# A decoder block's layer norm by running sums: statistics gathered per convolution group instead of after the convolution

## The chip, the cores and the metric

The kernel runs on one core of one Trainium2 chip. The metric is the device time of one execution in microseconds, lower is better. Five engines take part: TensorE (PE; its weight loads are PEld) multiplies matrices, VectorE (DVE) and ScalarE (ACT) work on elements, GpSimd (POOL) sets constants, and SyncE (SP) issues most of the loads. Every engine works through its own list of instructions in order and waits on semaphores for the others.

## What is computed

One hybrid decoder block over 256 tokens of 2048 channels. A combined projection feeds sparse attention and a causal convolution branch; both are gated, merged, projected by w_out and added to x through an adaLN gate g1; a gated MLP with a short convolution follows. The convolution branch is what the change touches:

```python
def conformer_conv(glu_in, w_dw, b_dw, ln_g, ln_b, w_pw, b_pw):
    a, g = jnp.split(glu_in, 2, axis=-1)
    u = a * jax.nn.sigmoid(g)
    u = causal_dwconv(u, w_dw, b_dw)                 # width 31, per channel
    u = jax.nn.silu(layernorm(u, ln_g, ln_b))        # over the 2048 channels of each token
    return u @ w_pw + b_pw

def layernorm(x, g, b):
    mu = jnp.mean(xf, axis=-1, keepdims=True)
    var = jnp.mean(jnp.square(xf - mu), axis=-1, keepdims=True)
    return (xf - mu) * lax.rsqrt(var + EPS) * g + b
```

## The kernel before

**Weight stream.** All large products run on weights streamed from memory in tiles of 128x1024 (512 KB). `wtile` (line 213) loads one into `raw` from SP's queue, ScalarE rounds it to `hi` (line 221), VectorE subtracts to get `lo` (line 222), and TensorE multiplies hi and lo parts with an activation that is split the same way (`split`, lines 344 and 345): 24 matmuls of 256 columns a tile in `sum_w` (lines 255 to 258), or as many of 512 columns for two tiles' worth of rows in `prod_x` (lines 243 to 245). There are four raw buffers and three each of hi and lo.

**Side work and its account.** Attention heads (`heads_q`), the convolution with its layer norm (`conv_q`) and the adaLN projections (`ada_q`) are queues of small steps. After each weight tile `tick` (line 122) adds to an account of each engine's time and gives out steps while no engine that the step costs is ahead of TensorE's account. A weight tile counts 2816 ns for TensorE (line 233) and 1217 for VectorE (line 223). `give` lets the step's instructions follow the `lo` of the tile before on VectorE (`issue_after`). `drain` gives all that is left. While `norm_only` is set and conv_q has steps, ada_q gets none.

**The convolution.** Channels lie in 16 blocks of 128 partitions; `u` holds all of them as [128, 16, 256]. Blocks are convolved in groups of three, the last one alone (`conv_blocks`, line 527): some taps are one VectorE instruction per block (line 543), the others a product on ScalarE per block (line 553) and one wide addition on VectorE for the group (line 562). The last addition writes the group back into u (line 560). The accumulator `cacc` has two buffers.

**The layer norm** comes after the last group, all through conv_q: `ln_mean1` to `ln_mean4` add the blocks up and a matmul with a matrix of ones sums over partitions; four `ln_centre` subtract the mean, square on ScalarE and fold (`half_sum`, lines 869 and 870); `ln_var` gets the reciprocal root; four `ln_scale` (line 917), eight `ln_silu` (line 923) and four `ln_split` end in uT, the activation of the next product, conv_pw_w (from line 961). Temporaries come from four buffers with the tag t4, also used by attention, by the products of the convolution and by the adaLN sums.

**What stands around it.** While the layer norm runs, TensorE does the products of the merge gates (line 952, four of eight tiles each). Then `drain(conv_q)`, the four products on conv_pw_w, and w_out in five chunks (line 1000) with `residual` behind each, which multiplies by g1b (line 990). g1b is the adaLN gate: 32 steps of ada_q, each a 512 KB piece of w_ada loaded into one of two `araw` buffers and a multiply-add on VectorE (lines 292 and 295), then products with ones and line 321. `conv_done` puts these 32 at the head of ada_q, since their result lies where the convolution's buffers were. What of them is left after the products on conv_pw_w is forced out by lines 972 and 973. Accumulators of w_out have two buffers, so the third chunk needs residual 0 done.

Of the kernel before, what the change touches and what calls it, by code (L numbers as in the profile page):

```python
# [9 lines left out]
F32 = mybir.dt.float32  # L10
F32R = mybir.dt.float32r
AF = mybir.ActivationFunctionType
ALU = mybir.AluOpType
# [3 lines left out]
P = 128  # L17
D = 2048
T = 256
# [12 lines left out]
EPS = 1e-6  # L32
# [15 lines left out]
LN_SILU = 1500  # L48
# [11 lines left out]
def block_kernel(ctx, tc, x, c, w_ada, b_ada, norm1_g, w_in, cmp_pe, w_kc1, w_kc2, w_vc1, w_vc2,  # L60
# [19 lines left out]
    def nm(s):  # L80
        n_[0] += 1
        return f"{s}_{n_[0]}"

    def t4(shape, dt=F32):
        return tmp.tile(shape, dt, tag="t4", name=nm("t4"))

    def pt(shape):
        return ps_t.tile(shape, F32, tag="pt", name=nm("pt"))
# [48 lines left out]
    def give(q):  # L137
        cost, f = q.popleft()
        use(**cost)
        with ExitStack() as es:  # L140
            es.enter_context(tc.issue_after(los[0]))
            if q is heads_q:
                es.enter_context(tc.high_priority(HP))
            f()

# [378 lines left out]

    MANY, FEW = tuple(s for s in range(2, CW) if s % 6) + (1,), tuple(range(6, CW, 4)) + (1,)

    def conv_blocks(b0, n, WIDE):

        box = {}
        blk = range(b0, b0 + n)  # L530

        def first(b):
            def f():
                if b == b0:
                    box["a"] = cvp.tile([P, n, T], F32, tag="cacc", name=nm("cacc"), bufs=2)
                nc.scalar.activation(box["a"][:, b - b0, :], u[:, b, :], AF.Identity, bias=cvb[:, b:b + 1],
                                     scale=cw[:, CW - 1, b:b + 1])
            return f

        def tap(b, s):  # L540
            def f():
                acc = box["a"][:, b - b0, s:]
                nc.vector.scalar_tensor_tensor(acc, u[:, b, :T - s], cw[:, CW - 1 - s, b:b + 1], acc,  # L543
                                               op0=ALU.mult, op1=ALU.add)
            return f

        def product(b, s):
            def f():
                if b == b0:
                    box["p"] = tmp.tile([P, n, T], F32, tag="t4", name=nm("cprod"))  # L550
                    if s == 1:
                        nc.gpsimd.memset(box["p"][:, :, 0:1], 0.0)
                nc.scalar.mul(box["p"][:, b - b0, s:], u[:, b, :T - s], cw[:, CW - 1 - s, b:b + 1])  # L553
            return f

        def wide(s):
            def f():
                acc, prod = box["a"], box["p"]
                if s == 1:
                    nc.vector.tensor_add(u[:, b0:b0 + n, :], acc, prod)  # L560
                else:
                    nc.vector.tensor_add(acc[:, :, s:], acc[:, :, s:], prod[:, :, s:])  # L562
            return f

        conv_q.extend(({"act": 600}, first(b)) for b in blk)
        narrow = deque(({"dve": 470}, tap(b, s)) for s in range(2, CW) if s not in WIDE for b in blk)
        each = -(-len(narrow) // len(WIDE))
        for s in WIDE:
            conv_q.extend(narrow.popleft() for _ in range(min(each, len(narrow))))
            conv_q.extend(({"act": 500}, product(b, s)) for b in blk)  # L570
            conv_q.append(({"dve": 170 + n * 265}, wide(s)))


    load.update(pe=0.0, dve=0.0, act=0.0, dma=0.0)
# [277 lines left out]
    def conv_done():  # L852

        cv.__exit__(None, None, None)
        norm_only[0] = True
        late = ctx.enter_context(tc.tile_pool(name="late", bufs=1))
        gate1["b"] = late.tile([P, D], F32, name="gb", tag="gb")
        gate1["rest"] = len(ada_q)
        for i in range(2):
            ada_q.extendleft(reversed(ada_steps(2 * D + i * WT, to_bcast(gate1["b"], 2 * D, i), 1500)))  # L860

    conv_q.append(({}, conv_done))


    lb = {}

    def half_sum(dst, a):

        nc.vector.tensor_add(a[:, 0:2, :], a[:, 0:2, :], a[:, 2:4, :])
        nc.vector.tensor_add(dst, a[:, 0, :], a[:, 1, :])  # L870

    def ln_mean1():
        lb["a"] = t4([P, 4, T])
        nc.vector.tensor_add(lb["a"], u[:, 0:4, :], u[:, 4:8, :])

    def ln_mean2():
        nc.vector.tensor_add(lb["a"], lb["a"], u[:, 8:12, :])

    def ln_mean3():
        nc.vector.tensor_add(lb["a"], lb["a"], u[:, 12:16, :])  # L880

    def ln_mean4():
        half_sum(lb["a"][:, 0, :], lb["a"])
        mp = pt([P, T])
        nc.tensor.matmul(mp, ones, lb["a"][:, 0, :], start=True, stop=True)
        lb["m"] = mp
        lb["q"] = t4([P, 4, T])

    def ln_centre(j):
        def f():  # L890
            v = u[:, 4 * j:4 * j + 4, :]
            nc.vector.scalar_tensor_tensor(v, lb["m"][:, None, :].to_broadcast([P, 4, T]), -1.0 / D, v,
                                           op0=ALU.mult, op1=ALU.add)
            s4 = t4([P, 4, T])
            nc.scalar.activation(s4, v, AF.Square)
            half_sum(lb["q"][:, j, :], s4)
        return f

    def ln_var():
        q = lb["q"]  # L900
        half_sum(q[:, 0, :], q)
        vp = pt([P, T])
        nc.tensor.matmul(vp, ones, q[:, 0, :], start=True, stop=True)
        ve = t4([P, 4, T])
        nc.vector.tensor_scalar(ve[:, 0, :], vp, 1.0 / D, EPS, op0=ALU.mult, op1=ALU.add)
        nc.scalar.activation(ve[:, 1, :], ve[:, 0, :], AF.Sqrt)
        nc.vector.reciprocal(ve[:, 2, :], ve[:, 1, :])
        nc.vector.tensor_mul(ve[:, 3, :], ve[:, 2, :], ve[:, 2, :])
        nc.vector.tensor_mul(ve[:, 3, :], ve[:, 3, :], ve[:, 0, :])
        nc.vector.tensor_scalar(ve[:, 3, :], ve[:, 3, :], -0.5, 1.5, op0=ALU.mult, op1=ALU.add)  # L910
        nc.vector.tensor_mul(ve[:, 3, :], ve[:, 3, :], ve[:, 2, :])
        lb["r"] = ve[:, 3, :]

    def ln_scale(j):
        def f():
            v = u[:, 4 * j:4 * j + 4, :]
            nc.vector.tensor_tensor(v, v, lb["r"][:, None, :].to_broadcast([P, 4, T]), op=ALU.mult)
        return f

# [6 lines left out]
    def ln_split(j):  # L926
        def f():
            if j == 0:
# [2 lines left out]
            split(lb["uT"][:, s], u[:, s, :])  # L931
        return f

    conv_q.extend(({"dve": d, "act": a}, f) for d, a, f in
                  [(1130, 0, ln_mean1), (1130, 0, ln_mean2), (1130, 0, ln_mean3), (900, 0, ln_mean4)]
                  + [(2000, 1050, ln_centre(j)) for j in range(4)] + [(3000, 1700, ln_var)]
                  + [(1130, 0, ln_scale(0))]
                  + [i for j in range(4) for i in [(1130, 0, ln_scale(j + 1))] * (j < 3)
                     + [(0, LN_SILU, ln_silu(4 * j)), (0, LN_SILU, ln_silu(4 * j + 2))]])


    merged = bigt([P, KB, T])
# [178 lines left out]
```

## Time and profile before

| | |
|---|---|
| runs | 1758.6, 1765.0, 1765.9 us (median 1765.0) |
| the profiled execution | 1765.5 us, span 1763.7 us |
| busy share of the span | PE 97%, PEld 88%, DVE 74%, ACT 56%, POOL 0% |
| mean granted TensorE clock | 0.98 |
| loads | 403 MB, 230 GB/s over the span |

The share of an engine is an average over the whole span; what matters for a change is the stretch where it acts. Here that is 227 us (the convolution starts) to 1000 us (w_out ends). The profile's page gives the shares, its lists name the waits, the windows give busy time and clock for a stretch, and the timelines show single instructions.

### The profile page before, as it was taken

The numbers are of one execution on the slowest core, as the hardware profiler recorded it, in microseconds if no ns is written. First come the engines' busy times: TensorE is split into PE (matmuls) and PEld (weight loads), VectorE is DVE, ScalarE is ACT, GpSimd is POOL, SyncE is SP. The second block draws the span as 40 slices with busy tenths as digits, with TensorE's granted clock in tenths as the row PEclk, the third lists the DMA queues.
The fourth block names the chain that finished last, engine by engine and source line by source line (L and its number), as shares of the span: only waits on it lengthen the run. The fifth ranks groups of instructions, "written<-read, shape, count | busy, mean of one in ns | idle before, by whom it ended". The sixth has DMA issues, their size and how long they took to land.

```text
span 1763.7 us, 29535 instructions
## 1 busy us (share of the span) xinstructions
PE 1703.1 (97%) x11652; PEld 1548.2 (88%) x11652; DVE 1313.1 (74%) x1722; ACT 991.5 (56%) x1506; POOL 6.2 (0%) x28
## 2 busy tenths in 40 slices
PE   6999999999999999996999899999999999999997
PEld 4899999999999999996987888888988888898886
DVE  2677798898887799887897677776577776576665
ACT  4443576885768767754434465554455554345553
POOL 0000000000000000000000000000000000000000
PEclk8999999999999999997999999999999999999998
DMA  9999788876556466767888667776777765666663
GB/s 343 328 350 318 240 272 273 268 247 217 157 174 185 143 212 202 221 217 274 305 296 308 199 216 226 226 225 221 224 225 220 223 211 183 191 191 188 188 193 124
DMA packets 263798, 406.82 MB, mean 231 GB/s; under 512 B 12620, under 2 KB 156780, under 8 KB 263020
## 3 DMA queue, kind: packets, MB, share of 16 engines
q1 hardware_dynamic: 261676, 399.44, 70.8%
q10 hardware_dynamic: 1984, 5.51, 0.9%
q8 instruction: 91, 1.49, 0.4%
q14 instruction: 47, 0.39, 0.1%
HBM read 402.80 MB, written 2.10 MB: 230 GB/s over the span
## 4 chain that ended last, share of the span: by engine, by line
PE 90%; DMA 5%; DVE 3%; issue 1%; ACT 1%; SPq 0%; DVEq 0%; ACTq 0%
PE accp L276 19%; PE accw L255 12%; PE accw L258 12%; PE accw L257 12%; PE accp L277 9%; PE accx L244 6%; PE accx L243 6%; PE accx L245 6%; DMA araw<-in_w_ada_dram 4%; PE pt L782 1%; DVE t L295 1%; PE pt L415 1%; PE pt L821 1%; DVE lo L222 1%; DMA araw<-in_w_kc_dram 1%
## 5 line engine op out<-in xcount | busy, mean ns | idle before, releaser
L221 ACT CAST hi<-raw 128x1024 fp32r<-128x1024 f32 x546 | 571.8, 1048 | 636.8 <-PE accw L257 196.9
L222 DVE TENSOR_TENSOR lo<-raw,hi 128x1024 fp32r<-128x1024 f32 x546 | 665.5, 1221 | 319.0 <-ACT hi L221 317.5
L255 PE MATMUL accw<-act,hi 128*128 128x256 f32 x1920 | 554.1, 289 | 21.7 <-ACT act L344 19.5
L257 PE MATMUL accw<-act,hi 128*128 128x256 f32 x1920 | 556.4, 290 | 1.5 <-DVE act L345 1.5
L258 PE MATMUL accw<-act,lo 128*128 128x256 f32 x1920 | 552.2, 288 | 0.7 <-DVE lo L222 0.7
L276 PE MATMUL accp<-act,hi 128*128 128x512 f32 x1408 | 492.3, 395 | 0.0
L255 PEld LDWEIGHTS accw<-act,hi 128*128 128x128 f32 x1920 | 374.0, 195 | 29.6 <-ACT act L344 21.0
L277 PE MATMUL accp<-act,lo 128*128 128x256 f32 x1408 | 393.3, 279 | 0.0
L257 PEld LDWEIGHTS accw<-act,hi 128*128 128x128 f32 x1920 | 373.8, 195 | 7.5 <-issue 4.9
L258 PEld LDWEIGHTS accw<-act,lo 128*128 128x128 f32 x1920 | 373.5, 195 | 6.8 <-issue 4.8
L276 PEld LDWEIGHTS accp<-act,hi 128*128 128x128 f32 x1408 | 264.0, 188 | 62.1 <-DVE act L345 0.3
L277 PEld LDWEIGHTS accp<-act,lo 128*128 128x128 f32 x1408 | 265.5, 189 | 0.2
L244 PE MATMUL accx<-lo,act 128*128 128x512 f32 (+2 forms) x664 | 228.9, 345 | 1.8 <-DVE lo L222 1.8
L243 PE MATMUL accx<-hi,act 128*128 128x512 f32 (+2 forms) x664 | 227.0, 342 | 0.0
L245 PE MATMUL accx<-hi,act 128*128 128x512 f32 (+2 forms) x664 | 226.8, 342 | 0.0
L295 DVE SCALAR_TENSOR_TENSOR t<-araw,cs,t 128x1024 f32<-128x1024 f32 x120 | 153.6, 1280 | 22.3 <-DMA araw<-in_w_ada_dram 22.0
L244 PEld LDWEIGHTS accx<-lo,act 128*128 128x128 f32 x664 | 125.8, 189 | 19.3 <-DVE lo L222 3.9
L243 PEld LDWEIGHTS accx<-hi,act 128*128 128x128 f32 x664 | 125.8, 189 | 14.6 <-issue 0.4
L245 PEld LDWEIGHTS accx<-hi,act 128*128 128x128 f32 x664 | 125.8, 189 | 14.6 <-issue 0.7
L553 ACT ACTIVATE cprod<-big,cw 128x230 f32<-128x230 f32 (+27 forms) x298 | 124.8, 486 | 11.1 <-DVE cacc L562 6.9
L562 DVE TENSOR_TENSOR cacc<-cacc,cprod 128x726 f32<-128x726 f32 (+28 forms) x110 | 87.5, 796 | 12.3 <-ACT cprod L553 9.6
L543 DVE SCALAR_TENSOR_TENSOR cacc<-big,cw,cacc 128x232 f32<-128x232 f32 (+24 forms) x182 | 77.4, 462 | 0.7
(205 smaller groups left out, 1036.8 us busy)
## 6 DMA issues: line engine op xcount, KB each, us to landing
araw<-in_w_ada_dram SPq DMA_DIRECT2D x192, 512.0 KB, 5.4
raw<-in_w_in_dram SPq DMA_DIRECT2D x180, 512.0 KB, 4.8
raw<-in_ffn_w_up_dram SPq DMA_DIRECT2D x176, 512.0 KB, 4.6
raw<-in_ffn_w_down_dram SPq DMA_DIRECT2D x88, 512.0 KB, 4.1
raw<-in_w_o_nsa_dram SPq DMA_DIRECT2D x32, 512.0 KB, 4.1
raw<-in_conv_pw_w_dram SPq DMA_DIRECT2D x32, 512.0 KB, 5.9
raw<-in_w_out_dram SPq DMA_DIRECT2D x32, 512.0 KB, 5.3
araw<-in_w_kc_dram SPq DMA_DIRECT2D x8, 512.0 KB, 6.3
```

What stands on the lines that cost most here:

```text
L221: nc.scalar.copy(hi[:, :n], raw[:, :n])
L222: los.append(nc.vector.tensor_tensor(lo[:, :n], raw[:, :n], hi[:, :n], op=ALU.subtract).ins)
L243: nc.tensor.matmul(o, act[:, k, 0, s], hi, start=k == 0, stop=False)
L244: nc.tensor.matmul(o, act[:, k, 0, s], lo, start=False, stop=False)
L245: nc.tensor.matmul(o, act[:, k, 1, s], hi, start=False, stop=k == nk - 1)
L255: nc.tensor.matmul(acc[:, b, :], hi[:, s], act[:, k, 0, :], start=begin and k == first and b % 2 == 0, stop=False, skip_group_check=True)
L257: nc.tensor.matmul(acc[:, b, :], hi[:, s], act[:, k, 1, :], start=False, stop=False, skip_group_check=True)
L258: nc.tensor.matmul(acc[:, b, :], lo[:, s], act[:, k, 0, :], start=False, stop=last, skip_group_check=True)
L276: nc.tensor.matmul(acc[:, b], hi[:, s], act[:, k], start=k == 0, stop=False, skip_group_check=True)
L277: nc.tensor.matmul(acc[:, b, 0, :], lo[:, s], act[:, k, 0, :], start=False, stop=k == KB - 1, skip_group_check=True)
L295: nc.vector.scalar_tensor_tensor(acc, raw, cs[:, k:k + 1], acc, op0=ALU.mult, op1=ALU.add)
L553: nc.scalar.mul(box["p"][:, b - b0, s:], u[:, b, :T - s], cw[:, CW - 1 - s, b:b + 1])
```

## The change

The layer norm's statistics are gathered as the convolution goes. `find` takes the mean over the first group before anything else as a `pivot` per token (sums on VectorE, a matmul with ones, a copy on ScalarE). For each group `less` subtracts the pivot from the group's blocks in u, and `add` squares them on ScalarE and adds blocks and squares, block by block, to two running sums in `sq`. After the last group `ln_var` sums both over partitions by one matmul with ones of 512 columns, and gets mean, variance as mean square less squared mean, and the reciprocal root. `ln_scale` now subtracts the mean and multiplies, four blocks at a time. The separate mean, centre and fold steps are gone.

Three more things change. cacc has one buffer, whose room sq and pivot take. conv_done, which puts the gate's steps into ada_q, now stands behind ln_var. norm_only is set in ln_var, and from then on steps of conv_q given by tick have the same high priority as attention heads. The costs of the steps in the account are new.

```diff
-            if q is heads_q:
+            if q is heads_q or q is conv_q and norm_only[0]:
                 es.enter_context(tc.high_priority(HP))
...
+    sq = cvp.tile([P, 2, T], F32, name="sq")
+    pivot = cvp.tile([P, T], F32, name="pivot")
+
+    def norm_sums(b0, n):
+        def sums(dst, a, fresh):
+            if fresh:
+                nc.vector.tensor_add(dst, a[:, 0, :], a[:, 1, :])
+            for j in range(2 if fresh else 0, n):
+                nc.vector.tensor_add(dst, dst, a[:, j, :])
+
+        def find():
+            sums(sq[:, 0, :], u[:, :n, :], True)
+            p_ = pt([P, T])
+            nc.tensor.matmul(p_, ones, sq[:, 0, :], start=True, stop=True)
+            nc.scalar.mul(pivot, p_, 1.0 / (n * P))
+
+        def less():
+            v = u[:, b0:b0 + n, :]
+            nc.vector.tensor_tensor(v, v, pivot[:, None, :].to_broadcast([P, n, T]), op=ALU.subtract)
+
+        def add():
+            v = u[:, b0:b0 + n, :]
+            s4 = t4([P, n, T])
+            nc.scalar.activation(s4, v, AF.Square)
+            sums(sq[:, 0, :], v, b0 == 0)
+            sums(sq[:, 1, :], s4, b0 == 0)
+
+        if b0 == 0:
+            conv_q.append(({"dve": 900, "act": 450, "pe": 250}, find))
+        conv_q.append(({"dve": 170 + n * 265}, less))
+        conv_q.append(({"dve": 840 * n, "act": 250 + 200 * n}, add))
...
-                    box["a"] = cvp.tile([P, n, T], F32, tag="cacc", name=nm("cacc"), bufs=2)
+                    box["a"] = cvp.tile([P, n, T], F32, tag="cacc", name=nm("cacc"))
...
             conv_q.append(({"dve": 170 + n * 265}, wide(s)))
+        norm_sums(b0, n)
...
     def conv_done():
         cv.__exit__(None, None, None)
-        norm_only[0] = True
...
-    conv_q.append(({}, conv_done))
...
-    def half_sum(dst, a): ...
-    def ln_mean1(): ...
-    def ln_mean2(): ...
-    def ln_mean3(): ...
-    def ln_mean4(): ...
-    def ln_centre(j): ...
...
     def ln_var():
-        q = lb["q"]
-        half_sum(q[:, 0, :], q)
-        vp = pt([P, T])
-        nc.tensor.matmul(vp, ones, q[:, 0, :], start=True, stop=True)
+        norm_only[0] = True
+        vp = pt([P, 2, T])
+        nc.tensor.matmul(vp.rearrange("p a t -> p (a t)"), ones, sq.rearrange("p a t -> p (a t)"), start=True, stop=True)
         ve = t4([P, 4, T])
-        nc.vector.tensor_scalar(ve[:, 0, :], vp, 1.0 / D, EPS, op0=ALU.mult, op1=ALU.add)
+        nc.vector.tensor_scalar(ve[:, 3, :], vp[:, 0, :], 1.0 / D, None, op0=ALU.mult)
+        nc.vector.tensor_mul(ve[:, 2, :], ve[:, 3, :], ve[:, 3, :])
+        nc.vector.scalar_tensor_tensor(ve[:, 0, :], vp[:, 1, :], 1.0 / D, ve[:, 2, :], op0=ALU.mult, op1=ALU.subtract)
+        nc.vector.tensor_scalar(ve[:, 0, :], ve[:, 0, :], EPS, None, op0=ALU.add)
...
     def ln_scale(j):
         def f():
             v = u[:, 4 * j:4 * j + 4, :]
+            nc.vector.tensor_tensor(v, v, lb["m"][:, None, :].to_broadcast([P, 4, T]), op=ALU.subtract)
             nc.vector.tensor_tensor(v, v, lb["r"][:, None, :].to_broadcast([P, 4, T]), op=ALU.mult)
...
+    conv_q.append(({"dve": 5500, "act": 500}, ln_var))
+    conv_q.append(({}, conv_done))
     conv_q.extend(({"dve": d, "act": a}, f) for d, a, f in
-                  [(1130, 0, ln_mean1), (1130, 0, ln_mean2), (1130, 0, ln_mean3), (900, 0, ln_mean4)]
-                  + [(2000, 1050, ln_centre(j)) for j in range(4)] + [(3000, 1700, ln_var)]
-                  + [(1130, 0, ln_scale(0))]
-                  + [i for j in range(4) for i in [(1130, 0, ln_scale(j + 1))] * (j < 3)
-                     + [(0, LN_SILU, ln_silu(4 * j)), (0, LN_SILU, ln_silu(4 * j + 2))]])
+                  [i for j in range(4) for i in [(2260, 0, ln_scale(j))]
+                   + [(0, LN_SILU, ln_silu(4 * j)), (0, LN_SILU, ln_silu(4 * j + 2))]])
```

## Rows read from the trace of the kernel before

**Rows 1.** The page's part 1: busy us (share of the span) xinstructions.

```profile
PE 1703.1 (97%) x11652; PEld 1548.2 (88%) x11652; DVE 1313.1 (74%) x1722; ACT 991.5 (56%) x1506; POOL 6.2 (0%) x28
```

**Rows 2.** Waits, 660 to 1000 us: us in total, times, longest us.

```profile
PE accw L255 <- ACT act L344: 17.7, 1, 17.7
...
PE accx L244 <- DVE lo L222: 1.8, 2, 1.1
```

**Rows 3.** Timeline of TensorE, 782 to 836: start, us, line, operation [idle before].

```profile
783.28 0.59 PE L903 MATMUL pt<-t,ones 128*128 128x256 f32 x2
...
789.82 0.28 PE L258 MATMUL accw<-act,lo 128*128 128x256 f32 x1
807.83 0.58 PE L255 MATMUL accw<-act,hi 128*128 128x256 f32 x1 [17.73 <-ACT act L344]
809.88 0.58 PE L257 MATMUL accw<-act,hi 128*128 128x256 f32 x1 [1.47 <-DVE act L345]
```

**Rows 4.** Windows: length, busy us (x) PE, PEld, DVE, ACT, POOL, PEclk, DMA, GB/s.

```profile
652.00:718.00 66.00, 66.00 (x554) 66.00 (x553) 60.47 (x71) 52.70 (x97) 0.10 (x1) 1.00 0.69 216
718.00:750.00 32.00, 32.00 (x269) 32.00 (x269) 26.67 (x42) 22.92 (x38) 0.10 (x1) 1.00 0.71 200
...
784.00:790.00 6.00, 6.00 (x51) 5.89 (x50) 5.09 (x5) 3.80 (x4) 0.00 (x0) 1.00 0.79 251
...
808.00:816.00 8.00, 6.53 (x29) 6.24 (x30) 6.42 (x6) 7.57 (x12) 0.00 (x0) 0.50 0.64 199
```

**Rows 5.** Chain of waits inside the gap: start us, us, what.

```profile
786.35 5.18 DMA araw<-in_w_ada_dram
```

**Rows 6.** Timeline of VectorE, 700 to 836 us.

```profile
730.98 1.39 DVE L562 TENSOR_TENSOR cacc<-cacc,cprod 128x249 f32<-128x249 f32 x3
...
750.27 0.42 DVE L560 TENSOR_TENSOR big<-cacc,cprod 128x256 f32<-128x256 f32 x1
...
782.05 1.23 DVE L222 TENSOR_TENSOR lo<-raw,hi 128x1024 fp32r<-128x1024 f32 x1 [1.32 <-ACT hi L221]
...
784.26 0.74 DVE L292 TENSOR_SCALAR t<-araw,cs 128x1024 f32<-128x1024 f32 x1
...
787.38 1.75 DVE L907 RECIPROCAL t<-t 128x256 f32<-128x256 f32 x1
...
801.54 4.63 DVE L917 TENSOR_TENSOR big<-big,t 128x1024 f32<-128x1024 f32 x4
```

**Rows 7.** VectorE's groups, 748 to 808 us: count | busy us, mean ns | idle before.

```profile
L917 DVE TENSOR_TENSOR big<-big,t 128x1024 f32<-128x1024 f32 x4 | 4.6, 1220 | 0.0
...
L869 DVE TENSOR_TENSOR t<-t 128x512 f32<-128x512 f32 x6 | 4.1, 688 | 0.1
L870 DVE TENSOR_TENSOR t<-t 128x256 f32<-128x256 f32 x6 | 2.5, 420 | 0.0
```

**Rows 8.** Timeline of ScalarE, 740 to 836 us.

```profile
785.34 1.28 ACT L906 ACT_TABLE_LOAD   x1
786.63 0.42 ACT L906 ACTIVATE t<-t 128x256 f32<-128x256 f32 x1
...
802.80 4.04 ACT L923 ACTIVATE big<-big,par 128x256 f32<-128x256 f32 x8 [7.79 <-DVE big L917]
806.75 1.03 ACT L344 CAST act<-big 128x1024 fp32r<-128x1024 f32 x1
```

**Rows 9.** Timeline of VectorE, 836 to 842 and 903 to 916 us.

```profile
838.00 1.22 DVE L222 TENSOR_TENSOR lo<-raw,hi 128x1024 fp32r<-128x1024 f32 x1
...
905.61 1.28 DVE L295 SCALAR_TENSOR_TENSOR t<-araw,cs,t 128x1024 f32<-128x1024 f32 x1
...
913.86 0.69 DVE L321 TENSOR_TENSOR gb<-pt,gb 128x512 f32<-128x512 f32 x1
```

**Rows 10.** Line 295 from 832 to 956 us: ns min/median/max, first and last start.

```profile
L295 DVE SCALAR_TENSOR_TENSOR t<-araw,cs,t x31: 1277/1283/1287, 832.2 to 951.3; 128x1024 f32<-128x1024 f32 x31
```

**Rows 11.** Timeline of TensorE, 954.5 to 958 us: the second w_out chunk's last matmul.

```profile
955.45 0.39 PE L245 MATMUL accx<-hi,act 128*128 128x512 f32 x1
```

More of the change, by code (lines that the diff above doesn't have):

```diff
@@ L860, in conv_done @@
             ada_q.extendleft(reversed(ada_steps(2 * D + i * WT, to_bcast(gate1["b"], 2 * D, i), 1500)))
-    conv_q.append(({}, conv_done))
     lb = {}
[L867 to L897, printed above, removed]
@@ L899, in ln_var @@
     def ln_var():
-        q = lb["q"]
-        half_sum(q[:, 0, :], q)
-        vp = pt([P, T])
-        nc.tensor.matmul(vp, ones, q[:, 0, :], start=True, stop=True)
+        norm_only[0] = True
+        vp = pt([P, 2, T])
+        nc.tensor.matmul(vp.rearrange("p a t -> p (a t)"), ones, sq.rearrange("p a t -> p (a t)"), start=True, stop=True)
         ve = t4([P, 4, T])
-        nc.vector.tensor_scalar(ve[:, 0, :], vp, 1.0 / D, EPS, op0=ALU.mult, op1=ALU.add)
-        nc.scalar.activation(ve[:, 1, :], ve[:, 0, :], AF.Sqrt)
@@ L907, in ln_var @@
[L907 to L912, printed above, removed]
+        nc.vector.tensor_scalar(ve[:, 3, :], vp[:, 0, :], 1.0 / D, None, op0=ALU.mult)
+        nc.vector.tensor_mul(ve[:, 2, :], ve[:, 3, :], ve[:, 3, :])
@@ new lines, in ln_var @@
+        nc.vector.scalar_tensor_tensor(ve[:, 0, :], vp[:, 1, :], 1.0 / D, ve[:, 2, :], op0=ALU.mult, op1=ALU.subtract)
+        nc.vector.tensor_scalar(ve[:, 0, :], ve[:, 0, :], EPS, None, op0=ALU.add)
+        nc.scalar.activation(ve[:, 2, :], ve[:, 0, :], AF.Sqrt)
+        nc.vector.reciprocal(ve[:, 1, :], ve[:, 2, :])
+        nc.vector.tensor_mul(ve[:, 2, :], ve[:, 1, :], ve[:, 1, :])
+        nc.vector.tensor_mul(ve[:, 2, :], ve[:, 2, :], ve[:, 0, :])
+        nc.vector.tensor_scalar(ve[:, 2, :], ve[:, 2, :], -0.5, 1.5, op0=ALU.mult, op1=ALU.add)
@@ L914, in ln_scale @@
+        nc.vector.tensor_mul(ve[:, 2, :], ve[:, 2, :], ve[:, 1, :])
+        lb["m"], lb["r"] = ve[:, 3, :], ve[:, 2, :]
     def ln_scale(j):
```

## The prediction

> **What bounds the kernel now.** I read the page first: TensorE is busy for 97% of the span [rows 1], so time can only be won where it stands still or runs slowly. The list of waits between 660 and 1000 us names one such place: 17.7 us for line 344, the cast that opens the split of the layer norm's result; the next one that I use below is 1.8 us [rows 2]. TensorE's timeline puts it in time: the last product of the gates ends at 790.1, the next starts at 807.83, is held once more for 1.47 us by line 345, and goes on at 809.88 [rows 3]. The windows give the clock: granted 1.00 (2.4 GHz) before the gap, with 51 matmuls in 6 us or 0.12 us each, and 0.50 (1.2 GHz) from 808 to 816 [rows 4]. There 29 matmuls take the 6.1 us from 809.88 on, 0.21 each, which loses 29 x 0.09 = 2.7 us. So the stop costs 17.7 + 1.5 + 2.7 = 22 us, the ceiling of what a shorter tail of the layer norm can give.
>
> The chain of waits shows what filled the gap: between the instructions of the variance stand loads of w_ada, one of them for 5.2 us [rows 5]. VectorE's timeline agrees: the convolution's last addition is at 750.27, the first step on w_ada for the gate at 784.26, the reciprocal of the variance at 787.38, and the four scalings start only at 801.54 [rows 6].
>
> **Removed.** From VectorE go three wide additions and four centrings (128x1024 like the scalings, 1.22 us each, 4.6 for four in a row) and the half sums (4.1 + 2.5): 3.6 + 4.6 + 6.6 = 14.8 us [rows 7].
>
> **Added ahead of the convolution's end.** Counted in the code: 32 additions of 128x256 (2 in find, 4 for the first group, 6 for each of four groups, 2 for the last) at 0.465 us, the pitch of dependent additions of that size (1.39 / 3, [rows 6]): 14.9 us; five subtractions of 128x768, estimated at 0.9 between the 128x512 and 128x1024 rows, and one of 0.42 [rows 7]: 4.9 us. Together 19.8 us. **Added in the tail**: four wide subtractions, 4.6 us like the scalings [rows 7], and three small instructions, 1.3. VectorE's net is 19.8 + 5.9 - 14.8 = +10.9 us. ScalarE squares as many elements as before and has one small copy more; TensorE's product with ones took 0.59 us for 256 columns [rows 3], and one of 256 and one of 512 stand for two of 256: 0.3 us more. Both hide behind the weight tiles and are costed at 0.3; uncovered they are worth 1 us.
>
> **Where the convolution's end goes.** In the account of tick each weight tile brings 2816 of TensorE and 1217 of VectorE, which leaves 1599 for queued steps. Ahead of the last addition now stand find (900), five less (965) and five add (2520): 18325, or 11.5 tiles. Following the account step by step, with the ada steps that take turns, it falls on weight tile 163 instead of 150 (the last of the gate products is 170). The trace runs behind the account: after 750.27 twelve tiles are left and not twenty, as the twelfth lo, at 782.05 [rows 6], is that of tile 170. With the same lag the end moves by 13 x 2.88 = 37 us, to 788. The bounds: the last group came at three additions a tile [rows 6], and its 25 would take 7 tiles instead of 10 if VectorE filled the 1.65 us that a tile leaves it, so 778 at the earliest; a bubble per group, because the one accumulator makes ScalarE wait for the last addition, gives 792. I take the middle, 785.
>
> **The tail behind it.** Clean: subtraction, square and two additions 1.7; matmul 1.1; four small instructions 1.6; Sqrt 0.8 with its hand-overs; reciprocal 1.75; four small ones 1.55; the first block's two wide instructions 2.3; four Silu 2.2; cast 1.1 [rows 3, 6, 7, 8]: 14.1 us. Up to three lo of 1.1 fall between; I add 2: 16 us. No gate step stands in it, since they are put off (below). TensorE restarts at 801 instead of 807.8: **-6.7 us**. The bounds are 794 (-13.8) and, from 792 with all three lo, 809.5 (+1.7). I leave the 1.5 and the 2.7 us behind the gap as they are.
>
> In the trace a table load of 1.28 us is followed by its activation at once (785.34 + 1.28, then 786.63), and ScalarE was ready for Silu 7.8 us before its data came [rows 8]. The Trainium skill, ScalarE: Activation LUTs, section What ACT_TABLE_LOAD costs, adds a drain of 1.38 us to each load, 2.66 for a switch. By that rule the tail's switches to Sqrt and Silu would make it 2.8 us longer and the gain here 3.9; these rows show no drain.
>
> **What is put off.** Until now gate steps (line 295 on w_ada columns for g1) were given from the last gate tile on, and the first ran inside the stop [rows 6]. After the change drain(conv_q) leaves VectorE's account 14.7 us above TensorE's, and tick gives the first one only with tile 182, in the second of the four products on conv_pw_w. In the trace the lo before it is at 838.00 [rows 9], 30 us after TensorE's restart S. All 32 must end before g1b is whole and residual 0 can free the accumulator that the third w_out chunk needs; the second chunk ended at 955.6 [rows 11], S + 148. One step came every 3.8 us (31 of line 295 and one first step from 832.2 to 951.3, [rows 10]), with two buffers that each wait for their load. Two are loaded ahead, so: S + 33 + 30 x 3.75 + 1.3 = S + 147; from the end of the last gate step to the end of line 321 took 7.7 us (906.9 to 914.55, [rows 9]), 2.5 if TensorE's four products with ones and the two additions come at once; two line 990, of 128x512, are 1.4 [rows 7]. That gives S + 151 to S + 156 against S + 148, a stop of 3 to 8 us: **+5 us** taken. At 3.2 us a step (load of 5.2 and step of 1.28, over two buffers [rows 5, 10]) it is nothing; at 3.9, the old gate steps' mean from 784.26 to 905.61 [rows 6, 9], and the long hand-over it is 12 and another 2.7 at 1.2 GHz. Nine of the 32 are no longer paced by tick but forced ahead of w_out; queued behind each one that waits for w_ada is, on VectorE, the lo of the next weight tile, and on SP, behind an araw buffer that is not free, the next weight load. The old kernel already lost 1.8 us to late lo there [rows 2].
>
> **The sum.** Against the profiled run's own 1765.5 us (span 1763.7): -6.7 + 5 + 0.3 = -1.4, so 1764 us. The median of the runs shown, 1765.0, is 0.5 us below the profiled run. A measurement of this kernel can tell about 0.5%, 9 us, from no change.
>
> **Rivals.** *The stop mostly vanishes.* VectorE stood idle for 10.9 of the 98 us between 652 and 750 [rows 4]; it takes the sums there and the convolution ends before 772. Then the drained steps come with the last tiles' lo, by 782, and the stop is 2 to 4 us: -14 to -16, and less by up to 2.7 if the clock stays up; with 0 to 5 for the gate 1747 to 1756, say 1751. For it: that idle time; against it: the account, not the engine, gives the steps out. Chance 0.22. *The gate comes late.* The same tail, but 3.9 us a step and the long hand-over, so that the third w_out chunk waits 12 us and runs 2.7 us at 1.2 GHz, and the forced steps double the 1.8 us of late lo: 1765.5 - 6.7 + 15 + 1.8 = 1776. It decides from the point where the last gate step ends after S + 145. For it: the pace in the rows; against it: with TensorE stopped, w_ada has the DMA to itself. Chance 0.20. *It doesn't do what it says.* The tail is merely moved: the convolution ends at 792 or later, the stop stays at 17 to 19 us and the gate costs 0 to 5: 1765 to 1771, say 1767. Chance 0.10.
>
> **How the numbers follow.** The forecast, 1764, has 0.48; its own bounds are 1754 to 1773. The range reaches into the two outer rivals and leaves about a tenth out on either side: 1750 to 1778. Faster by over 0.5% is the first rival, 0.22; slower is the second, 0.20; within 0.5% are the forecast and the third, 0.58.
>
> **What would show it.** Right: line 560's last addition near 785, TensorE's wait for line 344 near 11 us, no line 295 between 790 and 820, the first gate step some 30 us after S, and a wait of a few us before the third w_out chunk. Wrong: the last line 560 before 772 (then the lag is not what I took), a wait for line 344 under 4 us, a w_out without a gap (the steps' pace), or new waits of TensorE for lo between 300 and 750, which I cost at nothing because three lo buffers, 8.6 us of tiles, cover a late instruction; uncovered, each of the six groups could cost 1 us.

## The result and the profile after

The changed kernel takes **1779.6 us** (median; 1778.35 to 1783.71) against 1764.3 for the kernel before beside it (1758.62 to 1765.87): a ratio of 1.0097, 95% interval 1.0068 to 1.0125. It is slower by about 15 us, and lies 1.6 us above the range given. Its profiled execution took 1778.35 us with a span of 1776.6, 12.9 more than the span of before; what follows in this section accounts for those 12.9.

The page's part 1 of after (against [rows 1]): VectorE is busy for 6.9 us more, where 10.9 were forecast.

```profile
PE 1707.2 (96%) x11652; PEld 1548.6 (87%) x11652; DVE 1320.0 (74%) x1748; ACT 989.9 (56%) x1508; POOL 6.2 (0%) x28
```

The waits of after, 660 to 1000 us (against [rows 2]; total, times, longest). The stop at line 344 is 17.7 us as before, and there are two new waits: 5.1 us for line 993, the residual that needs the gate, and 2.7 us of the new product with ones for its sums.

```profile
PE accw L255 <- ACT act L344: 17.7, 1, 17.7
...
PE accx L243 <- DVE t L993: 5.1, 1, 5.1
...
PE pt L903 <- DVE sq L537: 2.7, 1, 2.7
```

TensorE's timeline of after (against [rows 3, 11]): the stop is in two parts, 2.71 and 17.73 us with the product with ones between them. The products of the gates end 2.71 us before 792.63, at 789.9, as in before (790.1), so that nothing of the 12.9 us was lost earlier. TensorE restarts at S = 812.43 instead of 807.83. The third w_out chunk begins at 966.16, and its first nine matmuls are 0.43 us apart.

```profile
792.63 2.07 PE L903 MATMUL pt<-sq,ones 128*128 128x512 f32 x2 [2.71 <-DVE sq L537]
812.43 0.58 PE L255 MATMUL accw<-act,hi 128*128 128x256 f32 x1 [17.73 <-ACT act L344]
...
966.16 0.76 PE L243 MATMUL accx<-hi,act 128*128 128x512 f32 x1 [5.13 <-DVE t L993]
966.72 0.63 PE L244 MATMUL accx<-lo,act 128*128 128x512 f32 x1
```

The windows of after (against [rows 4]; the granted clock is the third number from the end). Beside the convolution VectorE is 3.2 us busier than before (60.81 + 29.50 against 60.47 + 26.67). In the stop the granted clock is 0.50 (1.2 GHz), and the 5.8 us behind the new stop have 0.68.

```profile
652.00:718.00 66.00, 66.00 (x553) 66.00 (x552) 60.81 (x84) 41.58 (x69) 0.10 (x1) 1.00 0.70 220
718.00:750.00 32.00, 32.00 (x269) 32.00 (x268) 29.50 (x33) 27.15 (x51) 0.10 (x1) 1.00 0.71 210
...
800.00:812.00 12.00, 0.00 (x0) 0.00 (x0) 8.75 (x12) 7.58 (x12) 0.00 (x0) 0.50 0.00 1
...
966.20:972.00 5.80, 5.80 (x18) 4.63 (x19) 5.37 (x8) 2.82 (x6) 0.00 (x0) 0.68 0.77 238
```

VectorE's timeline of after (against [rows 6, 9]) holds the tail. The convolution's last addition is at 789.71 (before: 750.27). Between the four small instructions of the variance (L905 to L908) stand all four wide subtractions, two by two. The scalings begin at 806.14, the gate's first step is at 842.85, its last rows are summed at 965.93.

```profile
789.71 0.43 DVE L594 TENSOR_TENSOR big<-cacc,cprod 128x256 f32<-128x256 f32 x1
...
794.74 0.42 DVE L905 TENSOR_SCALAR t<-pt 128x256 f32<-128x256 f32 x1 [2.17 <-PE pt L903]
795.20 2.36 DVE L920 TENSOR_TENSOR big<-big,t 128x1024 f32<-128x1024 f32 x2
797.47 0.42 DVE L906 TENSOR_TENSOR t<-t 128x256 f32<-128x256 f32 x1
797.81 2.35 DVE L920 TENSOR_TENSOR big<-big,t 128x1024 f32<-128x1024 f32 x2
800.08 0.42 DVE L907 SCALAR_TENSOR_TENSOR t<-pt,t 128x256 f32<-128x256 f32 x1
800.53 0.29 DVE L908 TENSOR_SCALAR t<-t 128x256 f32<-128x256 f32 x1
802.65 1.75 DVE L910 RECIPROCAL t<-t 128x256 f32<-128x256 f32 x1 [1.82 <-ACT t L909]
...
806.14 4.63 DVE L921 TENSOR_TENSOR big<-big,t 128x1024 f32<-128x1024 f32 x4
...
842.85 0.75 DVE L292 TENSOR_SCALAR t<-araw,cs 128x1024 f32<-128x1024 f32 x1
...
965.93 0.68 DVE L321 TENSOR_TENSOR gb<-pt,gb 128x512 f32<-128x512 f32 x1
```

ScalarE's timeline of after (against [rows 8]): the table load of the square root begins only when its input is there, and eight Silu, not four, stand ahead of the first cast.

```profile
800.90 1.28 ACT L909 ACT_TABLE_LOAD   x1 [8.79 <-DVE t L908]
802.20 0.42 ACT L909 ACTIVATE t<-t 128x256 f32<-128x256 f32 x1
...
807.40 4.04 ACT L927 ACTIVATE big<-big,par 128x256 f32<-128x256 f32 x8 [3.49 <-DVE big L921]
811.35 1.03 ACT L344 CAST act<-big 128x1024 fp32r<-128x1024 f32 x1
```

**Where the 12.9 us are.** TensorE's next common mark behind w_out, the first transpose of h2, is at 1007.02 before and 1019.80 after. Of the 12.8 us between them 4.6 are the later restart (812.43 - 807.83) and 8.2 are lost between the restart and the mark (207.37 us against 199.19). So there are two questions: why the restart did not come earlier, and what the gate costs.

### The profile page after: what moved, and what is told of

It reads as the page before. It is cut to its first block, busy times and chain, and to the rows that moved or that the text cites. A ratio compares the mean times of both kernels' runs of the same rounds, so it can differ in the third digit from the quotient of the medians.

```text
span 1776.6 us, 29561 instructions
## 1 busy us (share of the span) xinstructions
PE 1707.2 (96%) x11652; PEld 1548.6 (87%) x11652; DVE 1320.0 (74%) x1748; ACT 989.9 (56%) x1508; POOL 6.2 (0%) x28
## 4 chain that ended last, share of the span: by engine, by line
PE 87%; DMA 6%; DVE 4%; issue 1%; ACT 1%; SPq 0%; DVEq 0%; ACTq 0%
PE accp L276 18%; PE accw L255 12%; PE accw L258 12%; PE accw L257 12%; PE accp L277 9%; PE accx L244 6%; PE accx L245 6%; PE accx L243 6%; DMA araw<-in_w_ada_dram 5%; DVE t L295 1%; PE pt L817 1%; PE pt L415 1%; DVE lo L222 1%; PE pt L856 1%; DMA araw<-in_w_kc_dram 1%
## 5 line engine op out<-in xcount | busy, mean ns | idle before, releaser
L255 PEld LDWEIGHTS accw<-act,hi 128*128 128x128 f32 x1920 | 372.8, 194 | 33.1 <-ACT act L344 23.1
```

What stands on the lines that cost most here:

```text
L255: nc.tensor.matmul(acc[:, b, :], hi[:, s], act[:, k, 0, :], start=begin and k == first and b % 2 == 0, stop=False, skip_group_check=True)
```

## Experiments

### The convolution's end: account, work, or accumulator

The prediction moved the convolution's end by the planner's account alone. Two runs part the account from the work, and a third the single accumulator from both.

**b_pace**, before with the account of the new steps and nothing of their work:

```
         conv_q.append(({"dve": 170 + n * 265}, wide(s)))
+    if b0 == 0:
+        conv_q.append(({"dve": 900, "act": 450, "pe": 250}, lambda: None))
+    conv_q.append(({"dve": 170 + n * 265}, lambda: None))
+    conv_q.append(({"dve": 840 * n, "act": 250 + 200 * n}, lambda: None))
```

> The kernel before, with steps that do nothing in conv_q where the change has find, less and add, at the same costs in the account. Theory A (the account sets where the convolution ends): the last addition of the convolution (750.3 us before, 789.7 after the change) comes at 784 to 792 although no engine has more to do; the old layer norm then starts there, its tail of some 30 us in a row puts TensorE's restart at 818 to 826, the gate steps come late as well, and the kernel takes 1783 to 1795 us. Theory B (VectorE's added 11 us of work set it): the last addition stays at 750 to 755 and the time at 1765.

**a_free**, after with find, less and add at `{"dve": 0}` in the account: the work without the account.

> The changed kernel with find, less and add counted as nothing in the account; the work is the same. Theory A: the convolution's last addition comes at 752 to 770, the variance and the split are done before or soon after the gate products end, TensorE's wait for line 344 is under 6 us, the gate steps start before the restart and there is no stop before the third w_out chunk: 1743 to 1757 us. Theory B: VectorE cannot do it sooner, the last addition stays at 783 to 792, and the time at 1772 to 1780.

**b_one**, before with `bufs=2` taken off the accumulator `cacc`.

> The kernel before with one accumulator buffer for the convolution's groups instead of two, nothing else. Theory A: ScalarE waits at each of six groups for the last addition of the group before, and VectorE idles: the last addition comes 1 to 4 us after the 750.27 of before, time 1765 to 1769. Rival B: products are given several tiles apart, the buffer is free in time: the last addition within 0.5 us of 750.27, time within 2 us of before.

b_pace took 1784.2 us (ratio 1.0103, 1.0088 to 1.0118), a_free 1776.8 (1.0063, 1.0048 to 1.0078), b_one 1772.3 (1.004, 1.0027 to 1.0053). VectorE's timelines of b_pace, a_free and b_one, one row each, give the convolution's last addition:

```profile
769.65 0.42 DVE L560 TENSOR_TENSOR big<-cacc,cprod 128x256 f32<-128x256 f32 x1
```

```profile
773.36 0.42 DVE L594 TENSOR_TENSOR big<-cacc,cprod 128x256 f32<-128x256 f32 x1
```

```profile
758.03 0.41 DVE L560 TENSOR_TENSOR big<-cacc,cprod 128x256 f32<-128x256 f32 x1
```

From 750.27 the account alone moves it by 19.4 us, work and accumulator together by 23.1, the accumulator alone by 7.8; after shows 39.4. So neither theory of the first two runs holds. By the prediction's reckoning the account gives the last addition out 13 tiles later in b_pace as in after, but in b_pace it runs only 6.7 tiles later (19.4 / 2.88), so that the lag of 8 tiles falls to under 2; in after it runs 13.7 tiles later (39.4 / 2.88), and the lag stays. That VectorE catches up in pauses that the sums fill in after is the likely reason, but no run shows it by itself. The parts do not add up either (19.4 + 23.1 against 39.4).

The single accumulator was expected to delay the last addition by 1 to 4 us or not at all, and delays it by 7.8; b_one as a whole is 7.1 us slower than before (1772.3 against 1765.2). Of the 6.9 us between the spans of the two traces 1.7 are there at TensorE's restart (809.50 against 807.83), although the stop is 1.7 us shorter (16.05); TensorE loses 2.7 us at the heads between 600 and 652 (busy 49.31 us, before 52.00). The other 5.2 come behind the restart. What makes the heads wait, and where those 5.2 arise, was not traced. In after sq and pivot take the room of the second accumulator, and no run gives it back there, so that the accumulator's share in after stays open.

The time of b_pace lies in theory A's range, but by another way than theory A's: TensorE restarts at 808.82, one us after before, and then waits 13.0 us for the gate, since its steps, too, were put off. The wait list of b_pace:

```profile
PE pt L320 <- DVE t L295: 13.0, 1, 13.0
```

a_free ends its convolution 16 us sooner than after and still gains only 2.7 us, so that its time lies in theory B's range although its convolution does not end where theory B has it. In its tail the gate's steps, lo tiles and the four wide subtractions all stand between the small instructions, from 780.10 to the scalings at 810.73, and TensorE restarts only at 817.01, after a stop of 15.89 us. What it takes to shorten that chain is the matter of the next two parts.

### The gate steps: in the tail, or late

Three versions of **before** give the gate's steps only when the layer norm is out, and differ in one number, how far VectorE's account then stands above TensorE's, that is, how late the steps come:

```
 def conv_done():
-    gate1["rest"] = len(ada_q)
-    for i in range(2):
-        ada_q.extendleft(...)
+    gate1["go"] = False
 ...
-    for q in (conv_q, ada_q)[:1 if norm_only[0] and conv_q else 2]:
+    for q in (conv_q, ada_q)[:1 if norm_only[0] and not gate1["go"] else 2]:
 ...
 drain(conv_q)
+gate1["go"], gate1["rest"] = True, len(ada_q)
+for i in range(2):
+    ada_q.extendleft(...)
+load["dve"] = min(load["dve"], load["pe"])      # b_hold
+load["dve"] = load["pe"] + 14700.0              # b_late
+load["dve"] = load["pe"] + 6000.0               # b_mid
```

> The kernel before with the 32 gate steps held back until the layer norm is all given out, and the VectorE account then put level with TensorE's. Theory A (the gate steps and their loads stretch the variance in the old tail): without them the way from line 905 to the scalings, 17.6 us, shrinks to 8 to 11, TensorE restarts at 798 to 802 instead of 807.8, the gate is ready in time, and the kernel takes 1755 to 1760 us. Rival: the tail is bound by VectorE's order, not by these steps: restart at 806 to 808, 1764 to 1767.

> As b_hold, but the VectorE account is put 14.7 us above TensorE's, which is where the changed kernel leaves it. Theory A (a late gate costs by itself): the same early restart as b_hold, but the first gate step 30 us after it, and TensorE waits 4 to 8 us for line 990 before the third w_out chunk; 7 to 10 us more than b_hold, 1763 to 1769. Rival (the stop in w_out of the changed kernel comes from the loads or from something else): no stop there, and within 2 us of b_hold.

> The kernel before with the gate steps held back until the layer norm is out and the VectorE account put 6 us (not 14.7, as in b_late) above TensorE's, so that the first gate step comes four weight tiles into the product behind the layer norm. Theory A (the gate steps cost twice: inside the tail by stretching it, and behind it by coming late; between the two lies room): restart of TensorE at 799 to 803 as in b_late (800.2), no stop before the third w_out chunk, 1757 to 1761 us. Rival (the scheduler moves them into the tail anyway, as in b_hold): restart at 806 and 1763.

b_hold took 1763.4 us (0.9989, 0.9979 to 0.9998), b_late 1767.2 (1.0016, 1.0004 to 1.0028), b_mid **1759.2** (0.997, 0.9958 to 0.9982). VectorE's timeline of b_hold shows steps on w_ada back in the tail, although the code gives them behind it: VectorE's list does not keep the order of the code here. So b_hold did not do what it was made for; TensorE restarts at 806.16, as its rival said, but because the steps had come back.

```profile
788.75 1.28 DVE L295 SCALAR_TENSOR_TENSOR t<-araw,cs,t 128x1024 f32<-128x1024 f32 x1 [0.77 <-DMA araw<-in_w_ada_dram]
789.95 1.22 DVE L222 TENSOR_TENSOR lo<-raw,hi 128x1024 fp32r<-128x1024 f32 x1
791.08 0.42 DVE L906 TENSOR_TENSOR t<-t 128x256 f32<-128x256 f32 x1
...
798.22 1.28 DVE L295 SCALAR_TENSOR_TENSOR t<-araw,cs,t 128x1024 f32<-128x1024 f32 x1 [2.02 <-DMA araw<-in_w_ada_dram]
...
799.87 4.63 DVE L915 TENSOR_TENSOR big<-big,t 128x1024 f32<-128x1024 f32 x4
```

In b_late the same stretch is free of them. From the variance's first instruction to the scalings it takes 9.1 us there and 17.1 in b_hold (782.77 to 799.87). VectorE's timeline of b_late:

```profile
784.07 0.42 DVE L903 TENSOR_SCALAR t<-pt 128x256 f32<-128x256 f32 x1 [0.64 <-PE pt L901]
...
793.17 4.63 DVE L915 TENSOR_TENSOR big<-big,t 128x1024 f32<-128x1024 f32 x4
```

So the gate's steps between the small instructions make up some 8 of the 17.7 us of the stop of before. TensorE's timeline of b_late: the stop is 9.95 us and the restart at 800.21, but the gate comes late, as in after and as theory A has it.

```profile
800.21 0.58 PE L255 MATMUL accw<-act,hi 128*128 128x256 f32 x1 [9.95 <-ACT act L344]
...
953.02 0.76 PE L243 MATMUL accx<-hi,act 128*128 128x512 f32 x1 [5.05 <-DVE t L992]
```

b_mid keeps the early restart (798.86) and has no wait for the gate. Between b_late and b_mid only the time of the gate steps differs, and the medians are 8.0 us apart. In the traces both stops are 9.95 us; b_late restarts 1.4 us later because its variance began that much later (784.07 against 782.72), which is no work of the gate steps. From the restart to the first transpose of h2 b_late takes 208.0 us (to 1008.21) and b_mid 199.1 (to 997.96), 8.9 more. The wait is 5.05 of them, and behind it the clock is at 1.2 GHz. The windows of b_late, then of b_mid: 14 matmuls in the same 5.8 us against 27, which at 0.22 us each is another 2.8.

```profile
953.00:958.80 5.80, 5.78 (x14) 4.55 (x15) 5.42 (x8) 2.90 (x7) 0.00 (x0) 0.50 0.75 226
```

```profile
953.00:958.80 5.80, 5.80 (x27) 4.82 (x26) 4.18 (x5) 1.21 (x2) 0.00 (x0) 1.00 1.01 354
```

So gate steps that come late cost 5.05 + 2.8 = 7.9 us by these rows, near the 8.2 that after loses behind its restart; the last 1.0 of the 8.9 is not placed. Behind the transpose b_mid is 1.9 us slower than b_late (759.1 against 757.2 us), which brings the spans to 8.3 apart; that was not traced.

### The tail of the changed kernel

**a_mid** is after with the edits of b_mid. **a_tail_mid** adds to it that the scaling is by the root first and then less mean times root, and that each block's split is queued right behind its Silu. **a_free_mid** is a_mid with a_free's account.

> The changed kernel with the same hold and 6 us. Theory A: restart of TensorE at 811 to 814 as after the change (812.4), the first gate step within 20 us of it, no stop before the third w_out chunk: 1769 to 1773 us, 7 to 10 less than the changed kernel. Rival (the loss in w_out has another cause): a stop there of 4 us or more, 1777 to 1781.

> a_mid, and the tail put in order: the scaling multiplies first and subtracts mean times reciprocal root, so that no wide subtraction is ready inside the chain of the variance; and each block's split is queued right behind its own Silu. Theory A (four subtractions put into the chain cost 3.4 to 4.5 us there, four Silu ahead of the first cast 2 us): restart 5 to 7 us earlier than a_mid, at 805 to 808, 1763 to 1768 us. Rival (the same work comes before the restart in any order): restart at 811 to 814, no gain on a_mid.

> a_mid with find, less and add counted as nothing in the account, that is a_free without gate steps in its tail. Theory A: convolution's last addition at 771 to 776 as in a_free (773.4); the chain from the first instruction of the variance to the scalings, 30 us in a_free, falls to 14 to 20 with only lo steps between; restart at 798 to 805 instead of 817; 1757 to 1765 us. Rival (lo steps alone stretch the chain as much): restart at 810 to 817, 1768 to 1776.

a_mid took 1773.6 us (1.005, 1.0033 to 1.0068), just above the 1769 to 1773 expected: 6.0 less than after, with no wait for the gate, and the restart still at 813.91, as theory A has it. a_tail_mid took 1773.5 (1.0049, 1.0033 to 1.0065), nothing gained, against 1763 to 1768 expected. VectorE's timeline of a_tail_mid says why: the four small instructions are now free of wide subtractions (794.04 to 796.24, with one first gate step of 0.74 us among them), but the multiplications of all four blocks come ahead of the first block's subtraction, and eight Silu still ahead of the cast. What left the variance came back behind it, and the restart is at 812.72.

```profile
801.56 1.22 DVE L919 TENSOR_TENSOR big<-big,t 128x1024 f32<-128x1024 f32 x1
802.70 0.42 DVE L913 TENSOR_TENSOR t<-t 128x256 f32<-128x256 f32 x1
803.03 3.49 DVE L919 TENSOR_TENSOR big<-big,t 128x1024 f32<-128x1024 f32 x3
806.44 4.62 DVE L920 TENSOR_TENSOR big<-big,t 128x1024 f32<-128x1024 f32 x4
```

a_free_mid took 1773.1 (1.0055, 1.0036 to 1.0074), 8 us above the upper end expected. Its convolution ends at 773, yet TensorE is held for 9.16 us until 809.15, for now six lo of 1.2 us come between the small instructions; L903 at 779.77 to L912 at 797.20 is 17.4 us, of which the wide subtractions have 4.6. ScalarE adds its part: behind the first four Silu (to 801.53) come a weight tile's cast, a Sigmoid of the gates with a table load of 1.28 us ahead of it and another behind it, and four more Silu, before the first cast starts at 808.07.

So the next runs fix the order itself. **a_order** is a_mid with the wide instructions behind the whole variance, block by block, each block's split queued right behind its Silu, and each block's Silu behind the cast of the block before (`issue_after` puts the instructions inside it behind the one named, on that engine; the operands are shortened here):

```
+with tc.issue_after(lb["last"]):
     nc.vector.tensor_tensor(v, v, m, op=ALU.subtract)
-    nc.vector.tensor_tensor(v, v, r, op=ALU.mult)
+    lb["last"] = nc.vector.tensor_tensor(v, v, r, op=ALU.mult).ins
 ...
+with tc.issue_after(lb["cast"]):      # the cast of the block before
     nc.scalar.activation(u[:, b, :], u[:, b, :], AF.Silu, ...)
```

**a_free_order** is the same on a_free_mid, and **b_order** the Silu's part on b_mid.

> The changed kernel as in a_mid (gate steps held back until the layer norm is out, account 6 us above TensorE's), and the tail in a fixed order: the wide subtractions only behind the whole variance, then subtraction and scaling block by block; the Silu of a block of four only behind the cast of the block before. Theory A: what is left of the stop is the order of the lists. In a_mid the four subtractions stand between L903 (795.69) and L906 (802.02), 6.3 us for four small instructions that take 1.8 without them; eight Silu (4.0 us) stand ahead of the first cast, of which four are enough. So -4.5, +1.2 for the first block's subtraction, -2.0: TensorE restarts 5.3 us earlier than in a_mid's profile, near 808.6, and the time is 1768 (1766 to 1770.5). Rival B: the order is a symptom, and the restart waits for table loads, hand-overs or a clock that is low anyway: restart 812 to 815, time 1772 to 1775.

> As a_order, and the sums, subtractions and squares of the convolution cost nothing in the account (as in a_free_mid, whose convolution ends at 773.4 and whose TensorE restarts at 809.15 after a stop of 9.16). Theory A: restart near 803, stop 3 to 4 us, time 1764 to 1769, the 6 us of the order taken off a_free_mid's 1773. Rival B: with TensorE still at work a lo comes between every two steps of the chain anyway, and the order buys less than 2 us: 1771 to 1774. Under both it stays above b_mid (1759), because heads and weight tiles lose a few us at 540 to 640, as in a_free_mid.

> b_mid (kernel before, gate steps held back, account 6 us above) with the Silu of a block of four only behind the cast of the block before, and each split queued right behind its Silu. Theory A: the first cast comes four Silu, 2.0 us, earlier: restart 796.8 instead of 798.86, time 1757.2 (1755.5 to 1758.5). Rival B: the later casts then come late instead, and TensorE waits the same 2 us at the second block: 1758.5 to 1760.

a_order took 1768.0 us (1.0026, 1.0014 to 1.0039), 5.6 less than a_mid, and 1768 was expected. Its profiled execution, 1764.23 us, is the fastest of its ten, so that its trace shows more of a gain than the medians do. Timelines of a_order, VectorE first, then ScalarE and TensorE: 7.4 us from the first small instruction to the first wide one (after: 11.4 to the scalings), then one block at a time, and four Silu.

```profile
792.40 0.42 DVE L903 TENSOR_SCALAR t<-pt 128x256 f32<-128x256 f32 x1 [1.22 <-PE pt L901]
...
799.80 1.22 DVE L919 TENSOR_TENSOR big<-big,t 128x1024 f32<-128x1024 f32 x1
801.05 1.22 DVE L920 TENSOR_TENSOR big<-big,t 128x1024 f32<-128x1024 f32 x1
```

```profile
802.31 2.08 ACT L929 ACTIVATE big<-big,par 128x256 f32<-128x256 f32 x4 [4.62 <-DVE big L920]
804.42 1.04 ACT L938 CAST act<-big 128x1024 fp32r<-128x1024 f32 x1
```

```profile
791.24 1.13 PE L901 MATMUL pt<-sq,ones 128*128 128x512 f32 x2 [2.71 <-DVE sq L537]
805.52 0.58 PE L255 MATMUL accw<-act,hi 128*128 128x256 f32 x1 [13.15 <-ACT act L938]
```

The same two rows of a_mid:

```profile
793.58 2.07 PE L901 MATMUL pt<-sq,ones 128*128 128x512 f32 x2 [2.71 <-DVE sq L537]
813.91 0.58 PE L255 MATMUL accw<-act,hi 128*128 128x256 f32 x1 [18.26 <-ACT act L344]
```

The restart is 8.4 us earlier than in a_mid. Of these it had 2.3 already at the last small addition of the sums (L537 at 790.76 against 793.10). Another 0.9 is the product with ones, which in a_order ran at a granted clock of 1.00 and in a_mid at 0.50, behind the same wait of 2.71 us; no edit did that. The other 5.1, from the first small instruction to the restart (13.1 us against 18.2), are the order's, and 5.3 were expected. Rival B, that the order is a symptom, is out. No run shows why the wide subtractions came between the small instructions in the first place: that they need only the mean is one reason, and the high priority that the change gives to steps of conv_q may be another; all runs on the changed kernel keep it.

a_free_order took **1760.8** us (0.9975, 0.9964 to 0.9985), below the range expected. TensorE's timeline of a_free_order:

```profile
803.47 0.39 PE L255 MATMUL accw<-act,hi 128*128 128x256 f32 x1 [0.55 <-ACT act L938]
804.92 0.39 PE L257 MATMUL accw<-act,hi 128*128 128x256 f32 x1 [1.06 <-DVE act L939]
```

The stop is gone, and with it the half clock (granted 1.00 from 803 to 816, where a_free_mid has 0.67 from 809 to 816). Its profiled execution took 1765.61 us, the slowest of its runs (from 1755.39), so that its trace shows 6.8 us of the 12 by which the medians of a_free_mid and a_free_order differ; the rest is not placed. The windows of a_free_order also show what the sums cost elsewhere: in 540 to 640 us, where the heads run, TensorE is busy for 95.17 of 100 us; in before it is 100.00.

```profile
540.00:640.00 100.00, 95.17 (x674) 87.17 (x674) 81.39 (x158) 73.49 (x172) 0.00 (x0) 0.98 0.48 158
```

b_order took 1760.4 us (0.9978, 0.9966 to 0.999), no gain on b_mid. The restart did come 3.2 us earlier (795.69); 1.8 of these are the shorter stop (8.13 against 9.95 us, where 2.0 was expected), the others were there before the variance began. But between 823 and 831 TensorE waits three times for a lo, 1.8 us in all, behind weight loads that came late. ScalarE's timeline of b_order, where the cast of a weight tile waits for its load while w_ada is read beside it:

```profile
821.02 1.05 ACT L221 CAST hi<-raw 128x1024 fp32r<-128x1024 f32 x1 [6.16 <-DMA raw<-in_conv_pw_w_dram]
```

So Rival B's total came out, by another way than it said. b_mid, which leaves the layer norm as it was, and a_free_order both beat the kernel before by 0.25 to 0.3%; between the two no difference is shown.

## Why the prediction was wrong

**What was right.** The place of the stop and its cost in before; that nothing is gained from VectorE's total; no step on w_ada between 790 and 820; the gate's first step 30.4 us behind the restart (30 forecast); the third w_out chunk at S + 153.7 (S + 151 to S + 156 forecast), with a stop of 5.13 us (5 taken); no new waits for lo worth naming between 300 and 750.

**The convolution's end: 785 taken, 789.7 measured**, inside its bounds of 778 to 792. That it came so near is in part luck. The step said that the account moves the end by 37 us and the lag stays. b_pace shows 19.4 for the account alone. The other 20 came with things to which the prediction gave no time beyond its bounds: the work of the sums, and the single accumulator (7.8 us in b_one, where the bound allowed 4). How the 20 divide between them in after is not shown.

**The tail: 16 us taken, 22.3 measured** (790.14, the end of the last addition, to 812.43). This is the step that failed: with its 6.3 us back the time, some 1773, would lie inside the range. The forecast of the profiled execution was off by 14.3 us (-1.4 forecast, +12.9 measured): 6.3 in the tail, 5.1 in the convolution's end (785 to 790.14) and 3.2 in the gate, less the 0.3 taken for uncovered work. The tail's terms, forecast and measured in after:

| term | forecast | after | from |
|---|---|---|---|
| subtraction, square, two sums, and a lo | 1.7 + 2 reserved | 2.5 | 790.14 to 792.63 |
| product with ones | 1.1 | 2.1 | 792.63 to 794.74 |
| four small instructions | 1.6 | 6.1 | 794.74 to 800.82 |
| Sqrt and hand-overs | 0.8 | 1.8 | 800.82 to 802.65 |
| reciprocal and four small | 3.3 | 3.5 | 802.65 to 806.14 |
| first block's wide work | 2.3 | 1.3 | 806.14 to 807.40 |
| Silu | 2.2 | 3.9 | 807.40 to 811.35 |
| cast | 1.1 | 1.1 | 811.35 to 812.43 |

Four terms make it up, and what was reserved for lo tiles or moved elsewhere gives back 2. The **four wide subtractions** (4.5 us) were counted for one block, between variance and Silu; but they need only the mean, and all four were laid between the instructions of the chain. The **eight Silu** (1.7 us more than four) stood in a quoted row: [rows 8] shows eight of them, 4.04 us, ahead of the cast at 806.75, and the prediction wrote four. The **Sqrt** was costed at 0.8 with its hand-overs; its table load of 1.28 us was put at nothing without a reason, but it begins only when its input is there and is on the path (1.0 more). The **product with ones** ran at 1.2 GHz, 2.07 us instead of 1.1; in a_order it took 1.13 at 2.4 GHz, so that this 1.0 is not in every execution. a_order confirms the first two together: 4.5 + 1.7 - 1.2 for the first block's own subtraction, which comes back onto the path, is 5.0, and it gained 5.1.

In after the table load of the square root (800.90 + 1.28) is followed by its activation at 802.20, and in a_order by the same 0.02 us (794.68 + 1.28, 795.98). The Trainium skill, ScalarE: Activation LUTs, section What ACT_TABLE_LOAD costs, adds a drain of 1.38 us at every switch to a different set; the rows here show none, and the miss of 1.0 in that term is the load's own time.

**The gate: 5 taken, 8.2 measured.** The stop was as forecast. What was left out is what the rival's price had, the clock behind it: nine matmuls 0.43 us apart instead of the 0.22 of the rows ahead of the stop, 1.9 us. The other 1.2 us between restart and mark are not placed.

**The range.** The sum's worst restart was 809.5 and its worst gate belonged to a rival that kept the good tail. After has a restart 2.9 us beyond the first bound and half of the second's loss, and no case held both. The third rival, the tail merely moved, described the stop of 17.7 us rightly, though the convolution ended before its 792, and gave the gate only 0 to 5.

**The idea itself.** Of the 17.7 us of the stop of before, 7.8 came from the gate's steps between the variance's instructions and not from the layer norm's own passes: b_late and b_mid keep those passes and cut the stop to 9.95 us by moving the steps alone. The change moved the steps too, and so late that they cost 8 us elsewhere, while its own wide subtractions took their place in the tail. The running sums do remove the stop once the account and the order are set right as well (a_free_order), but by then the time is no better than b_mid's, which has no running sums.

## What to carry to other kernels

When a chain of small dependent instructions sets the end, list every independent instruction on the same engine that can start by then and ask which of them will be laid between its links; removing one kind only makes room for the next, so fix the order, as in a_order, before counting on a shorter chain. A planner's account does not tell by itself when a step runs: in b_pace 13 tiles in the account became 6.7 in the trace. When a step is put off, find the point where it becomes late, and price the wait with the slow clock behind it. Count the instructions ahead of a hand-over from the row that shows them (x8), not from the code that needs four.

## What the runs showed of the hardware

After a stop of 5.13 us TensorE came back at 1.2 GHz: the window behind it shows a granted clock of 0.68, and nine matmuls at about twice their usual distance. The waits of 0.55 and 1.06 us in a_free_order had no such cost: the granted clock behind them is 1.00, 2.4 GHz. A wait of 2.71 us went either way: the product with ones behind it took 2.07 us at a granted 0.50 in after and in a_mid, and 1.13 at 1.00 in a_order (1.12 in a_tail_mid). And in b_order, with the gate's loads and the weights read together, one load of conv_pw_w came 6.2 us after ScalarE was free for it.
